# Five edits to a decoder layer's schedule: prepared weights, first differences, first sums, attention's merge, output steps

## The chip, the cores and the metric

The kernel runs on one core of a Trainium2 chip. The time is that of one execution of the whole program on the device, in microseconds. The engines that matter are TensorE (PE: matrix products and transposes), VectorE (DVE), ScalarE (ACT), GpSimd (POOL) and SyncE (SP), which here only issues transfers; ACT and POOL issue transfers too, between their computing instructions. [...]

## The reference

One layer of a decoder on 1024 positions of width 1024, in float32: half a SwiGLU block, a mixer of two groups of heads (stick-breaking attention and a Mamba-2 scan) side by side, cross-attention to 256 memory tokens, and a second half SwiGLU block, each between two RMS norms:

```
f = swiglu(rmsnorm(h, ffn1_pre_g), ffn1_w_gu, ffn1_w_down)
h = h + 0.5 * rmsnorm(f, ffn1_post_g)
m = hybrid_mixer(rmsnorm(h, mix_pre_g), w_in, ...)        # attention heads | SSD heads
h = h + rmsnorm(m, mix_post_g)
c = memory_cross_attention(rmsnorm(h, xa_pre_g), rmsnorm(mem, mem_g), ...)
h = h + rmsnorm(c, xa_post_g)
f = swiglu(rmsnorm(h, ffn2_pre_g), ffn2_w_gu, ffn2_w_down)
h = h + 0.5 * rmsnorm(f, ffn2_post_g)
```

## The kernel before

**Arithmetic.** Every float32 matrix is split into a high part (`hi`, a cast on ACT, L266) and a low part (`lo`, a subtraction on DVE, L268), and a product is three matmuls per block of 128 rows: high by high, high by low, low by high (`mm3`). The feed-forward blocks are computed with Strassen's seven products: `seven(f)` (L799) makes 7 products of 12 matmuls each for one tile `f` of the hidden width, in the order B22, B21, S1, S4, B12, S5, B11. The sums of weight blocks are formed on POOL (`wc`, L754), then split on ACT and DVE; their buffers (2 in the first block, 3 in the second) come free when the low part is made. Between the products the results are combined: ACT copies the first two (L808, L812), POOL subtracts them (L813), DVE adds the third to form `e` (L818). The sixth product, S5, accumulates in the bank that L818 reads, so PE starts it only after L818.

**The order of the work.** The program is written along PE's order. `clock` adds up the modelled cost of the matmuls traced so far, in ns; `later` is a list of steps with a due time on that clock, and `run_later` traces each step when PE's clock passes its time. A step traced in this way is kept behind the instruction traced just before it on its engine (`kp`). A scheduler then sets the final order of each engine. `merge(a, ta, b, tb)` interleaves two strands on PE: it advances `a` as long as (clock spent in a) / ta is not above (clock spent in b) / tb.

**Names and places that the change touches.**

- `prepare` (L191 on): weights for later stages are loaded in halves, split, and stored again as `dwhi` and `dwlo`, in steps `load`, `high` (ACT, L212), `low` (DVE, L216) and `store` (two transfers, L220). `prepare_all` (L241) sets the due times for 74 halves: one every 4300 from 152000 while below 416000 (62 halves), the other 12 every 9000 from 420000. Times below 418000 use SP's queue, later ones POOL's.
- `pair_sums(f, ...)` (L637): five sums over the tiles f-1 and f are made on DVE (L643); each is stored by a transfer from ACT's queue (L645) that is due 2500 later. At f = 5 in the second feed-forward block the first of them is due 4000 later than elsewhere.
- `last(k)` (L723): in the first feed-forward block it splits the four matrices B12, one cast on ACT and one subtraction on DVE each. They are due at 0, 800, 1600 and 2400 after the start of the first `seven` (L922).
- In attention, `tail()` is the last head pair (scores, scans on DVE, transposes, products with the values) and `beside()` is the first part of the output projection followed by the values of the memory tokens (`memory_values`). L1901 merges them with 32500 and 21000 + 5200 * 6 = 52200. After it come two weight tiles of the output projection whose halves were prepared, and `mix_out`, which loads the attention's result (`oraw`), splits it (`ohi`, `olo`) and sums its squares (`asum`).
- In cross-attention, at step s = 6 (L2168), the softmax and value steps of one head are merged with the first eight steps of two output tiles (`out_parts`), with weights 6100 and 5200.

Of the kernel before, what the change touches and what calls it, by code (L numbers as in the profile page):

```python
# [10 lines left out]
F32 = mybir.dt.float32  # L11
# [14 lines left out]
MIXED = 6  # L26
# [21 lines left out]
class Kern:  # L48
# [142 lines left out]
    def prepare(self, names, raw, pairs, times, switch=float("inf")):  # L191


        nc = self.nc
        work = []
        for name, i in names:
            hl = tuple(self.tc.dram_tile([P, KT, P], F32R, name=self.nm(n)) for n in ("dwhi", "dwlo"))
            self.ready[name, i] = hl
            work += [(self.ap["w_" + name][i], hl, slice(4 * n, 4 * n + 4)) for n in range(2)]
        raws, parts = {}, {}  # L200

        def queue(n):
            return nc.sync if times[n] < switch else nc.gpsimd

        def load(n):
            pool, tag, bufs = raw[n % len(raw)]
            raws[n] = self.t(pool, [P, 4, P], F32, tag, bufs=bufs)
            self.kp(queue(n).dma_start(out=raws[n], in_=work[n][0][:, work[n][2], :]))

        def high(n):  # L210
            parts[n] = [self.t(pool, [P, 4, P], F32R, tag, bufs=bufs) for pool, tag, bufs in pairs[n % len(pairs)]]
            self.kp(nc.scalar.copy(parts[n][0], raws[n]))  # L212

        def low(n):
            hi, lo = parts[n]
            self.kp(nc.vector.tensor_tensor(out=lo, in0=raws.pop(n), in1=hi.bitcast(F32), op=ALU.subtract))  # L216

        def store(n):
            for d, x in zip(work[n][1], parts.pop(n)):
                self.kp(queue(n).dma_start(out=d[:, work[n][2], :].bitcast(F32), in_=x.bitcast(F32)))  # L220

        if len(pairs) > 2:
            steps = ((low, -1, 0), (store, -2, 0), (high, 0, 0), (load, 2, 0))
        else:
            steps = ((high, 0, 0), (low, 0, 1200), (load, 2, 2400), (store, 0, 3000))
        times = list(times)[: len(work)]
        assert len(times) == len(work), (len(times), len(work))
        d = times[1] - times[0]
        times = {n: t for n, t in enumerate(times)}
        times.update({-n: times[0] - d * n for n in (1, 2)})  # L230
        times.update({len(work) + n: times[len(work) - 1] + d * (n + 1) for n in range(2)})
        for n in sorted(times):
            for f, m, dt in steps:
                if 0 <= n + m < len(work):
                    self.later.append((times[n] + dt, lambda f=f, m=n + m: f(m)))

# [4 lines left out]
    def prepare_all(self, sp):  # L241
        names = [("ssd", i) for i in [*range(6), *range(12, 26)]] + [("qkv", i) for i in range(QKV)]
        pairs = [
            ((self.fp, "acc0", None), (self.fp, "acc1", None)), ((self.fp, "rpost", None), (self.tp, "dg", None)),
            ((sp, "bh", None), (sp, "bl", None)),
        ]
        raw = [(sp, "braw", 2), (sp, "braw", 2), (self.xp, "xl0", KT + 1), (self.xp, "xl1", KT + 1)]
        n = 2 * len(names)
        a = [152000 + 4300 * i for i in range(n)]
        k = sum(t < 416000 for t in a)  # L250
        self.prepare(names, raw, pairs, a[:k] + [420000 + 9000 * i for i in range(n - k)], 418000)

    def wsrc(self, name, i):
        return self.ready[name, i] if (name, i) in self.ready else self.ap["w_" + name][i]
# [306 lines left out]
    def up_phase(self, sp, sp2, wgu, gpre, act_d, bank, load, plain, sizes, rw=None, begin=None):  # L561

        nc = self.nc
# [10 lines left out]
        if begin:  # L574
            x = sums(F32)
# [15 lines left out]
        xs_d, stored, later_sums, held = {}, [0] * (NFF // 2), [], []  # L591
# [45 lines left out]
        def pair_sums(f, even, odd):  # L637

            (t0, t1), (u0, u1) = even, odd
            j, c = f // 2, self.clock + (4000 if f == 5 and not begin else 0)  # L640

            def combine(n, out, a, b, op):
                self.kp(nc.vector.tensor_tensor(out=out, in0=a, in1=b, op=op))  # L643
                xs_d[n, j] = self.tc.dram_tile([P, H], F32, name=self.nm("xs"))
                at(self.clock + 2500, lambda: self.kp(nc.scalar.dma_start(out=xs_d[n, j], in_=out)))  # L645

            def fresh(n, a, b, op):
                combine(n, self.t(ftp, [P, H], F32, "cb", bufs=3), a, b, op)

            if c == self.clock:  # L650
                fresh("s6", t1, t0, ALU.subtract)
            else:
                at(c, fresh, "s6", t1, t0, ALU.subtract)
            at(c + 1500, fresh, "s5", t0, u0, ALU.add)
            at(c + 5000, combine, "s1", t0, t0, u1, ALU.add)
            at(c + 6500, combine, "s7", u0, u0, u1, ALU.subtract)
            at(c + 8000, combine, "s2", t1, t1, u1, ALU.add)
# [81 lines left out]
        def at(t, f, *args):  # L739
            self.later.append((t, lambda: f(*args)))  # L740
# [111 lines left out]
        t0, dt = (T0 + 12000, 7000) if begin else (T0 + 31000, 6500)  # L852
# [66 lines left out]
                        at(self.clock + 1000, next, Wb)  # L919
        for k in range(4):  # L920

            at(self.clock + (800 * k if begin else 1500 * k + 500), last, k)  # L922
        for f in range(first_seven, NFF):
            seven(f)
        if not begin:
# [662 lines left out]
    def attention(self):  # L1588
        nc, ap = self.nc, self.ap
        with self.pools("at", ["o", "a"], ["w"]) as (op, sp, wsp, pp):  # L1590
# [12 lines left out]
            begin = self.t(op, [P, S], BF16, "begin")  # L1603
# [4 lines left out]
            for hh in range(2):  # L1608
                nc.vector.tensor_scalar(
                    out=sc[:, 4 * hh : 4 * hh + 4], in0=self.C[hh], scalar1=-0.125, scalar2=None, op0=ALU.mult  # L1610
# [268 lines left out]
            def tail():  # L1879
                yield from units(7)  # L1880
                yield from values(*pend.pop())
                yield from drain(0)

            def beside():
                late.append(mix_row(1))
                self.first = self.mix_first(ready.pop())
                for n in range(4 * MIXED):
                    if n == 2:
                        late.pop()()
                    if n == 4 * MIXED - 4:  # L1890
                        ready.append(next(Wm))
                    next(self.first)
                    yield
                yield from memory_values(*mem_prep())
# [3 lines left out]
            self.Wo, self.mix_r, ready, late = self.wstream(wo[0:MIXED]), [], [], []  # L1898
            for p in range(7):
                self.merge(units(p), 24000, inproj(p + 1), 32500)  # L1900
            self.merge(tail(), 32500, beside(), 21000 + 5200 * MIXED)  # L1901
            self.Wo = self.wstream(wo[MIXED:])
            with self.pinned(self.clock + 2500):
                vout(*pend_v.pop(0))
# [123 lines left out]
    def xattn(self):  # L2028


        nc = self.nc
        with self.pools("xf", ["a", "b", "w"], []) as (sp, sp2, wsp, pp):
# [87 lines left out]
            def out_parts(k0, k1, n=2):  # L2120
                for i in range(n):
                    yield from out_part(ps[i], ws[i], 1, k0, k1)
# [11 lines left out]
            fill = qproj(1)  # L2134
# [3 lines left out]
            for s in range(8):  # L2138
                hh = s // 4
                if s == 2:  # L2140
                    self.resid(0, 4000)
                if s == 4:
                    self.F[0] = []
                    for d in range(8):
                        ps = self.t(self.mmp, [P, H], F32, "mm")
                        self.run_all(out_part(ps, next(W), 0, 0, 8))
                        out_copy(ps, 0)
                    self.run_later(float("inf"))
                    self.post(0, "xa_post_g", None, "ffn2_pre_g", step=5000, at=(8500, 16000, 19000))
                if s == 3:  # L2150
                    self.run_later(self.clock)
                if s + 2 < 8:
                    load(K, s + 2, "k", 2, 0)
                if s == 6:
                    self.resid(1, 4000)
                if s == 2:
                    self.flush(1)
                    self.later.append((self.clock + 10000, self.held.pop()))
                    self.prepare([("gu2", i) for i in range(2 * PLAIN[1])], *self.prep_pool(wsp), [self.clock + 9000 + 6000 * i for i in range(4 * PLAIN[1])])
                if s < 7:  # L2160
                    step = zip_(values(s), scores(s + 1))
                    if s < 6:
                        fill = qproj(s + 2)
                        for _ in range(4):
                            next(fill)
                        self.merge(step, 6100, fill, 8300)
                    else:
                        self.F[1] = []  # L2168
                        ws = [next(W) for _ in range(2)]
                        ps = [self.t(self.mmp, [P, H], F32, "mm") for _ in range(2)]  # L2170
                        self.merge(step, 6100, out_parts(0, 4), 5200)
                    load(V, s + 1, "v", 1, 1)
            v = values(7)
            self.run_all(out_part(ps[0], ws[0], 1, 4, 6))
# [4 lines left out]
            for d in range(8):  # L2179
# [3 lines left out]
                else:  # L2183
                    x = self.t(self.mmp, [P, H], F32, "mm")
# [187 lines left out]
```

## Time and profile before

| | |
|---|---|
| time, median of 3 runs (lowest to highest) | 2639.64 us (2636.35 to 2641.0) |
| time of the profiled execution | 2638.67 us |
| its span, first to last instruction | 2636.9 us |
| busy ACT, share of the span | 1293.0 us, 49% |
| mean granted TensorE clock | 0.995 |
| transfers | 489.82 MB, mean 186 GB/s |

In the views below, a row of a timeline gives the start and the duration in us, the engine (a trailing q: a transfer is issued), the line of the kernel, the operation, the tiles as out<-in, the shape and the count; in brackets stands how long the engine sat idle before it, and what ended that. A row of the waits gives who waited for whom, the total in us, how often, and the longest. A row of the windows gives a stretch, its length, the busy time of each engine with its instruction count, the TensorE clock that was granted (1.00 is full), the busy share of the transfer engines and GB/s.

### The profile page before, as it was taken

What the parts mean: (1) busy time and instruction counts of PE and PEld (TensorE: products, weight loads), DVE (VectorE), ACT (ScalarE), POOL (GpSimd) and SP (SyncE); (2) the same over time, 40 slices, a digit from 0 to 9 for tenths busy, and PEclk for the clock granted to TensorE, in tenths of its full rate; (3) what the DMA queues carried; (4) which work ended last, traced back from release to release, by engine and by line L of the source; (5) the groups of instructions that cost most, each with busy time, mean ns of one, the idle gap of its engine ahead of it and who ended that gap; (6) DMA issues with size and microseconds to landing.
All of it is one profiled execution on the core that took longest, in us unless ns stands there. A gap on an engine that the chain in (4) does not pass through costs nothing. (4 is left out here: it accounts for less than half of the span.)

```text
span 2636.9 us, 36866 instructions
## 1 busy us (share of the span) xinstructions
PE 2586.9 (98%) x12850; PEld 2153.9 (82%) x12850; DVE 1981.5 (75%) x3044; ACT 1293.0 (49%) x2300; POOL 601.8 (23%) x717
## 2 busy tenths in 40 slices
PE   9999999999999999999999999999999999999999
PEld 7788888778777778888888887788878788888887
DVE  6778897769689784777777867767556888776777
ACT  7434444545356563555555645345554433333553
POOL 2555553110100001111111110101011555452000
PEclk9999999999999999999999999999999999999999
DMA  6558888875654226555555556547658453336554
GB/s 219 175 193 279 283 278 290 279 248 183 229 183 168 86 75 214 166 151 149 148 149 126 155 155 219 184 148 252 200 179 294 142 178 116 97 99 224 192 170 154
DMA packets 212970, 489.82 MB, mean 186 GB/s; under 512 B 26544, under 2 KB 35120, under 8 KB 212784
## 3 DMA queue, kind: packets, MB, share of 16 engines
q1 hardware_dynamic: 162896, 369.48, 42.9%
q0 software_dynamic: 26560, 75.52, 9.7%
q10 hardware_dynamic: 23328, 42.48, 4.3%
q8 instruction: 101, 1.65, 0.3%
q14 instruction: 85, 0.70, 0.1%
HBM read 327.46 MB, written 138.94 MB: 177 GB/s over the span
## 5 line engine op out<-in xcount | busy, mean ns | idle before, releaser
L139 PE MATMUL mm<-xh,whi 128*128 128x512 f32 x1320 | 520.9, 404 | 2.6 <-DVE xl L1929 1.6
L139 PE MATMUL mm<-xh,wlo 128*128 128x512 f32 x1272 | 488.7, 391 | 1.9 <-DMA wlo<-dwlo 1.9
L139 PE MATMUL mm<-xl,whi 128*128 128x512 f32 (+1 forms) x1252 | 486.6, 389 | 0.3 <-DVE xl L275 0.3
L139 PEld LDWEIGHTS mm<-xh,whi 128*128 128x128 f32 x1320 | 248.2, 188 | 44.9 <-issue 3.8
L139 PEld LDWEIGHTS mm<-xh,wlo 128*128 128x128 f32 x1272 | 238.8, 188 | 54.6 <-DMA wlo<-dwlo 2.3
L139 PEld LDWEIGHTS mm<-xl,whi 128*128 128x128 f32 x1252 | 236.2, 189 | 33.3 <-DVE xl L275 0.6
L1761 DVE TENSOR_TENSOR_SCAN nb<-nb,begin 128x128 f32<-128x128 f32 (+7 forms) x128 | 171.1, 1351 | 55.4 <-ACT nb L1757 54.7
L1757 ACT ACTIVATE nb<-z,scale 128x128 f32<-128x128 f32 (+2 forms) x192 | 107.7, 580 | 73.9 <-PE z L139 73.6
L268 DVE TENSOR_TENSOR wlo<-wraw,whi 128x1024 fp32r<-128x1024 f32 x70 | 85.4, 1221 | 55.8 <-ACT whi L266 55.6
L266 ACT CAST whi<-wraw 128x1024 fp32r<-128x1024 f32 (+1 forms) x87 | 84.0, 965 | 83.5 <-PE mm L139 55.3
L1778 POOL DMA_DIRECT2D mix<-sq x64 | 52.9, 826 | 227.4 <-DVE sq L1776 180.7
L139 PE MATMUL dn<-xh,wlo 128*128 128x512 f32 x296 | 101.8, 392 | 2.0 <-DMA wlo<-dwlo 2.0
L661 ACT ACTIVATE ft<-ft 128x512 f32<-128x512 f32 x88 | 55.5, 632 | 97.2 <-DVE ft L660 95.2
L754 POOL TENSOR_TENSOR wc<-wraw,raw 128x512 f32<-128x512 f32 x56 | 79.8, 1425 | 65.8 <-DVE whi L268 19.5
L754 POOL TENSOR_TENSOR wc<-raw,wraw 128x512 f32<-128x512 f32 x55 | 80.3, 1459 | 51.6 <-DVE blk L268 21.6
L268 DVE TENSOR_TENSOR atl<-tr,ath 128x512 fp32r<-128x512 f32 (+1 forms) x106 | 66.4, 630 | 28.6 <-ACT ath L266 28.2
L839 POOL TENSOR_TENSOR ft<-ft,e 128x512 f32<-128x512 f32 x37 | 59.4, 1606 | 121.4 <-DVE e L838 45.0
L139 PE MATMUL mm<-ath,v 128*128 128x256 f32 x320 | 85.3, 289 | 0.0
L139 PE MATMUL dn<-xh,blk 128*128 128x512 f32 x264 | 85.2, 389 | 0.0
L266 ACT CAST whi<-wc 128x512 fp32r<-128x512 f32 x80 | 49.7, 621 | 71.1 <-PE dn L139 25.9
L266 ACT CAST wlo<-wc 128x512 fp32r<-128x512 f32 x79 | 49.1, 621 | 72.0 <-PE dn L139 27.2
L139 PE MATMUL dn<-xh,whi 128*128 128x512 f32 x240 | 83.9, 394 | 0.0
(584 smaller groups left out, 6811.2 us busy)
## 6 DMA issues: line engine op xcount, KB each, us to landing
whi<-dwhi SPq DMA_DIRECT2D x82, 512.0 KB, 3.6
wlo<-dwlo SPq DMA_DIRECT2D x82, 512.0 KB, 4.9
wraw<-in_w_gu SPq DMA_DIRECT2D x43, 512.0 KB, 4.3
raw<-in_w_gu SPq DMA_DIRECT2D x37, 512.0 KB, 4.2
dwhi<-bh SPq DMA_DIRECT2D x66, 256.0 KB, 4.1
dwlo<-bl SPq DMA_DIRECT2D x66, 256.0 KB, 4.3
wraw<-xs SPq DMA_DIRECT2D x56, 256.0 KB, 3.1
xs<-ft ACTq DMA_DIRECT2D x54, 256.0 KB, 3.4
```

The lines of the kernel that those rows point to most:

```text
L139: self._pe(self.nc.tensor.matmul(out, lhsT, rhs, start=start, stop=stop, skip_group_check=self.more), cost)
L266: self.kp(self.nc.scalar.copy(hi, src))
L268: self.nc.vector.tensor_tensor(out=lo, in0=src, in1=hi.bitcast(F32), op=ALU.subtract)
L661: nc.scalar.activation(t, t, AF.Silu)
L754: nc.gpsimd.tensor_tensor(out=t, in0=a, in1=b, op=op)
L839: nc.gpsimd.tensor_tensor(out=t1, in0=t1, in1=e, op=ALU.mult)
L1757: nc.scalar.activation(nb[:, s0:s1], z[:, 0:n], AF.Sigmoid, scale=sc[:, i : i + 1])
L1761: nc.vector.tensor_tensor_scan(out=nb[:, 0:Wd][:, ::-1], data0=nb[:, 0:Wd][:, ::-1], data1=begin[:, S - Wd : S][:, ::-1], initial=0.0, op0 ...
L1778: nc.gpsimd.dma_start(out=self.mix_d[p][a * 64 : a * 64 + 64, csl], in_=o, accum_op=ALU.add)
```

## The change

Five places are edited; no operation of the computation is added or left out.

1. A prepared half's two stores become two steps. For the 12 halves after 416000 (now 9) the second store is due 3000 after the first and the next load 6000 after; before that, and in the preparations with two buffer pairs, the order is as it was. The spacing becomes 4100 instead of 4300 (65 halves), then 12000 instead of 9000.
2. The transfers of the sums at f = 5 of the second feed-forward block are due 5000 after their sums instead of 2500.
3. The four splits of B12 in the first feed-forward block are due at 3000, 4500, 6000 and 7500 after the start of the first `seven`.
4. Attention's last merge weighs `tail()` with 26000 instead of 32500.
5. At s = 6 of cross-attention two of the eight output steps are traced ahead of the merge, and the rest is weighed with 4000.

```diff
-        def store(n):
-            for d, x in zip(work[n][1], parts.pop(n)):
-                self.kp(queue(n).dma_start(out=d[:, work[n][2], :].bitcast(F32), in_=x.bitcast(F32)))
+        def st0(n):
+            store(n, 0)
+
+        def st1(n):
+            store(n, 1)
+
+        def store(n, i):
+            d, x = work[n][1][i], parts[n][i]
+            self.kp(queue(n).dma_start(out=d[:, work[n][2], :].bitcast(F32), in_=x.bitcast(F32)))
 
         if len(pairs) > 2:
-            steps = ((low, -1, 0), (store, -2, 0), (high, 0, 0), (load, 2, 0))
+            steps = ((low, -1, 0), (st0, -2, 0), (st1, -2, 3000), (high, 0, 0), (load, 2, 6000))
         else:
-            steps = ((high, 0, 0), (low, 0, 1200), (load, 2, 2400), (store, 0, 3000))
+            steps = ((high, 0, 0), (low, 0, 1200), (load, 2, 2400), (st0, 0, 3000), (st1, 0, 3000))
...
         for n in sorted(times):
             for f, m, dt in steps:
+                if len(pairs) > 2 and times[n] < switch:
+                    dt = 0
...
-        a = [152000 + 4300 * i for i in range(n)]
+        a = [152000 + 4100 * i for i in range(n)]
         k = sum(t < 416000 for t in a)
-        self.prepare(names, raw, pairs, a[:k] + [420000 + 9000 * i for i in range(n - k)], 418000)
+        self.prepare(names, raw, pairs, a[:k] + [420000 + 12000 * i for i in range(n - k)], 418000)
...
-            j, c = f // 2, self.clock + (4000 if f == 5 and not begin else 0)
+            j, wait = f // 2, (5000 if f == 5 and not begin else 2500)
+            c = self.clock + (4000 if wait == 5000 else 0)
...
-                at(self.clock + 2500, lambda: self.kp(nc.scalar.dma_start(out=xs_d[n, j], in_=out)))
+                at(self.clock + wait, lambda: self.kp(nc.scalar.dma_start(out=xs_d[n, j], in_=out)))
...
-            at(self.clock + (800 * k if begin else 1500 * k + 500), last, k)
+            at(self.clock + (3000 + 1500 * k if begin else 1500 * k + 500), last, k)
...
-            self.merge(tail(), 32500, beside(), 21000 + 5200 * MIXED)
+            self.merge(tail(), 26000, beside(), 21000 + 5200 * MIXED)
...
-                        self.merge(step, 6100, out_parts(0, 4), 5200)
+                        fill = out_parts(0, 4)
+                        for _ in range(2):
+                            next(fill)
+                        self.merge(step, 6100, fill, 4000)
```

## The prediction

> **What bounds the kernel now.** I read the page's shares first, then PE's waits over the whole execution, then the granted clock of short stretches.
>
> ```profile
> span 2636.9 us, 36866 instructions
> PE 2586.9 (98%) x12850; PEld 2153.9 (82%) x12850; DVE 1981.5 (75%) x3044; ACT 1293.0 (49%) x2300; POOL 601.8 (23%) x717
> ```
>
> TensorE is the bound: 50.0 us of the span are not busy. The diff removes no matmul, so it can only shorten PE's waits, and stretches in which PE runs at a lower clock. The waits at the five edited places:
>
> ```profile
> PE dn L139 <- DVE e L818: 5.9, 2, 5.6
> PE dn L139 <- ACT F L1079: 3.6, 1, 3.6
> PE mm L139 <- DVE e L818: 3.1, 2, 2.8
> PE dn L139 <- ACT F L1074: 2.7, 1, 2.7
> PE ms L139 <- DVE atl L268: 2.6, 1, 2.6
> PE tr L142 <- DVE p L2077: 2.2, 2, 1.2
> PE dn L139 <- ACT ohi L273: 2.0, 1, 2.0
> PE mm L139 <- DMA wlo<-dwlo: 1.9, 1, 1.9
> PE ms L139 <- DVE asum L1953: 1.4, 1, 1.4
> PE dn L139 <- DVE olo L275: 0.6, 2, 0.3
> ```
>
> By place, from the timeline: 5.6 at 100.5 us (first `seven`); 2.8 at 2102 (f = 5 of the second block); 2.7 at 484 and 3.6 at 550 (first down projection); 2.6, 1.9, 2.0, 0.6 and 1.4 between 1536 and 1600 (attention's end); 1.2 at 1918 (cross-attention). Behind most of them PE is slow for a while, as the windows show:
>
> ```profile
> 99.00:105.90 6.90, 5.40 (x13) 4.24 (x14) 6.90 (x9) 3.01 (x5) 4.52 (x4) 0.51 0.17 58
> 484.70:488.20 3.50, 3.50 (x9) 2.76 (x10) 3.50 (x7) 2.85 (x6) 0.00 (x0) 0.51 0.53 149
> 1600.80:1604.30 3.50, 3.50 (x9) 2.73 (x10) 3.50 (x7) 3.00 (x5) 0.00 (x0) 0.51 0.73 228
> 2102.60:2106.10 3.50, 3.50 (x11) 2.69 (x9) 3.50 (x6) 0.63 (x1) 2.58 (x2) 0.51 0.05 19
> 1536.00:1539.50 3.50, 2.82 (x24) 2.83 (x25) 1.78 (x4) 1.39 (x4) 0.00 (x0) 1.00 0.52 150
> 152.00:416.00 264.00, 264.00 (x1166) 218.62 (x1165) 226.59 (x299) 118.91 (x207) 153.73 (x99) 1.00 0.76 262
> 416.00:484.00 68.00, 65.92 (x291) 54.24 (x289) 51.31 (x77) 32.68 (x58) 13.44 (x15) 1.00 0.94 326
> 1564.00:1596.00 32.00, 27.77 (x152) 23.09 (x150) 16.48 (x26) 13.90 (x24) 5.22 (x9) 1.00 0.94 316
> ```
>
> The column ahead of the last two is the granted clock. At 0.51, 3.5 us lose 3.5 × 0.49 = 1.7; the 5.40 busy us behind the longest wait lose 2.6. The 2.6 us wait at 1536 was followed by full clock, so a wait of that size stands at the edge. Between 152 and 416 us PE is never idle: 264.00 us for 1166 matmuls, 0.226 us each. All touched places together: 5.6 + 2.6 at 100; 2.8 + 1.7 at 2102; 2.7 + 3.6 + 2 × 1.7 = 9.7 in the down projection (two clock losses); 2.6 + 1.9 + 2.0 + 0.6 + 1.4 + 1.7 = 10.2 at attention's end; 1.2 at 1918. That is 33.8 us, the most that can be won directly.
>
> **Part by part: splits of B12 (edit 3).** The timeline before the 5.6 us wait, start and duration first:
>
> ```profile
> 89.89 0.68 DVE L268 TENSOR_TENSOR xl<-braw,xh 128x512 fp32r<-128x512 f32 x1
> 90.71 0.63 ACT L266 CAST wlo<-wc 128x512 fp32r<-128x512 f32 x1
> 91.70 0.68 DVE L268 TENSOR_TENSOR xl<-cb,xh 128x512 fp32r<-128x512 f32 x1
> 92.30 0.68 DVE L268 TENSOR_TENSOR wlo<-wc,wlo 128x512 fp32r<-128x512 f32 x1
> 93.06 1.68 POOL L754 TENSOR_TENSOR wc<-raw 128x512 f32<-128x512 f32 x1 [4.24 <-DVE wlo L268]
> 95.92 1.72 POOL L813 TENSOR_TENSOR sq<-sq,sq 128x512 f32<-128x512 f32 x1
> 96.43 1.75 DVE L268 TENSOR_TENSOR blk<-wraw,blk 128x512 fp32r<-128x512 f32 x1
> 99.77 0.68 DVE L818 TENSOR_TENSOR e<-sq,dn 128x512 f32<-128x512 f32 x1
> ```
>
> PE waits for `e` (99.77), which stands behind the low parts of weight sums in DVE's queue; those stand behind POOL, which had idled 4.24 us for a buffer that the low part at 92.30 frees. Ahead of that low part DVE makes the four `xl` of B12, 89.89 to 91.70: 0.60 us apart, 4 × 0.60 = 2.4. Due at 3000 to 7500, all four fall behind it, and B12 is read only by the fifth product, so POOL starts 2.4 earlier. Everything behind moves with it: the wait becomes 3.2, and the clock loss one usual 1.7 less a part of it (1.3 of the 2.6 goes): −3.7. Ends: the whole place, −8.2; or the four lows run beside POOL, where the low at 96.43 takes 1.75 instead of 0.68 us: 4 × 1.07 − 2.4 = +1.9. I take −3.7, nearest to the rows as they stand. [...]
>
> **Stores of first sums (edit 2).** At 2102:
>
> ```profile
> 2094.66 1.62 POOL L839 TENSOR_TENSOR ft<-ft,e 128x512 f32<-128x512 f32 x1 [2.67 <-ACT blk L266]
> 2096.24 3.42 POOL L754 TENSOR_TENSOR wc<-raw 128x512 f32<-128x512 f32 x2
> 2099.63 1.71 POOL L813 TENSOR_TENSOR sq<-sq,sq 128x512 f32<-128x512 f32 x1
> 2100.67 0.62 ACT L266 CAST whi<-wc 128x512 fp32r<-128x512 f32 x1 [3.71 <-DVE cb L643]
> 2101.38 0.69 DVE L818 TENSOR_TENSOR e<-sq,mm 128x512 f32<-128x512 f32 x1 [1.16 <-POOL sq L813]
> ```
>
> The store of `cb` holds ACT's queue 3.71 us for the sum, and the edit frees it. But `e` is released by POOL's L813, and POOL works from 2094.66 to 2101.34 (2099.63 + 1.71) without a gap. Value 0: POOL hides it. If ACT's casts were the true releaser, −4.5 (2.8 + 1.7). If the later stores keep a `cb` buffer 2.5 us longer and DVE's next sum stands in front of `e`, +2.5.
>
> **Attention's merge (edit 4).** I replayed the order that the rule of L1901 gives, each step by its count of matmuls (0.226 us for 512 columns, half for 256). With 32500 the tail ends 7.1 us before the stage; with 26000 the output projection and the memory values go ahead, and the tail ends last, its 16 last products with only 2 us of other work before them. The memory's weights are asked for and used about 4 us earlier in the stage.
>
> ```profile
> L139 PE MATMUL mm<-atl,v x56: 276/283/287, 1475.0 to 1563.2; 128*128 128x256 f32 x56
> 1570.45 0.59 SPq L182 DMA_DIRECT2D wlo<-dwlo  x1
> L268 DVE TENSOR_TENSOR atl<-tr,ath 128x512 fp32r<-128x512 f32 (+1 forms) x106 | 66.4, 630 | 28.6 <-ACT ath L266 28.2
> raw<-in_w_gu SPq DMA_DIRECT2D x37, 512.0 KB, 4.2
> ```
>
> (a) At 1536 a row product waits for a bank that an `atl` reads. In the replay it comes 2.6 instead of 0.8 us behind the transposes into that bank: −1.8. (b) The weights asked for at 1570.45 land 3.9 later; such a load lands in 4.2 (last row). Issued 4 us earlier against the first use, its wait goes, up to a rest where the transfer engines are 0.94 busy: −1.7 of 1.9. (c) `oraw`, `ohi`, `olo` and `asum` follow on the same queues: I let −1.9 of 2.6 and −0.7 of 1.4 go, since a share of 0.94 leaves little room. (d) The clock loss at 1600.8 goes with them: −1.5 of 1.7. (e) New: the last transposes of the tail are followed by their cast and `atl` (0.63 by its row, and about as much for the cast) and then products with 2 us of cover; I charge +1.5. Sum −6.1. Ends: −10.2 with all gone; +3.2 where nothing goes and the tail's last chain is uncovered twice over (1.5 + 1.7 clock loss).
>
> **Output steps in front (edit 5).** At 1918:
>
> ```profile
> 1917.35 1.21 DVE L268 TENSOR_TENSOR wlo<-wraw,whi 128x1024 fp32r<-128x1024 f32 x1
> ```
>
> A transpose waits 1.2 for `p`, which stands behind this low part on DVE. Two steps, 6 matmuls × 0.226 = 1.36 us, now stand ahead of it: −1.1. Ends −1.2 and, if the steps are missed at the end of the merge, +1.2.
>
> **Prepared weights (edit 1).** Up to 416 us: 264 / 4.1 against 264 / 4.3 gives 3 more halves of 768 KB where PE has no wait: 0. After it, 9 halves instead of 12, with the stores apart. The two waits hang on late weights:
>
> ```profile
> 545.04 0.69 DVE L1022 TENSOR_TENSOR cb<-wraw,xl 128x512 f32<-128x512 f32 x1 [2.19 <-DMA wraw<-in_w_dn]
> SPq L220 <- DVE dg L216: 38.8, 12, 10.7
> ```
>
> A weight transfer now stands behind one piece of 256 KB instead of three; at the 326 GB/s of 416 to 484 us a piece takes 0.8. That moves the 550 wait by at most 1.6, and I take half: −0.8. The 484 wait is ACT's own queue and stays. Ends: −9.7 (both with their clock), and +8.3 (the slower rival's single event below).
>
> Sum: −3.7 + 0 − 6.1 − 1.1 − 0.8 = −11.7. The profiled execution took 2638.67 (span 2636.9 and 1.8 around it), 0.97 under the median of 2639.64, so the forecast is 2638.67 − 11.7 = 2627.0.
>
> **Rivals.** *The orders resolve their places fully.* Edit 3 brings −8.2 and edit 4 −7.8 (as above without the two rests, 0.2 and 1.5), edit 5 −1.2, edit 1 −0.8, edit 2 −4.5: −22.5, 2616. For it: a wait below 2.6 brings no clock loss, so gains double near that edge. Against: POOL's gapless row at 2094.66.
>
> *VectorE and GpSimd slow each other.* The B12 lows run beside POOL and give edit 3 back (+1.9): −11.7 + 3.7 + 1.9 = −6.1, 2632.6. For it: 1.75 at 96.43; against: POOL's idle 4.24 shows that there was room. [...]
>
> *Nothing much happens.* Edit 4's stretch is bound by its transfers (0.94) and gives 0; edit 3 moves only two splits past the low part, −1.2; edit 5 −1.1: 2636.4.
>
> *Slower: prepared stores hold the weight queue.* SP's queue takes its transfers in order, and between 152 and 416 us it held 12 times for the low part of a prepared half (last row above), up to 10.7 us. Weight loads of the feed-forward stand behind those stores. At 4100 they fall at other points of the 84-matmul tile (84 × 0.226 = 19.0 us). Two longest holds in a row, 21.4, and 4.2 of landing exceed the 19.0 by 6.6; with 1.7 of clock loss that is 8.3 an event. From two longest holds back to back on it decides. Three such events, +24.9 − 11.7: 2651.9. For it: the denser spacing and the DMA share of 0.76; against: 264.00 us without one wait.
>
> **How the numbers follow.** Forecast 0.36 (its own range 2618 to 2634); full resolution 0.16; contention 0.10; nothing much 0.16; slower 0.22 (with one event 2635, three 2652). About 0.2%, or 5.3 us, can be told from no change: faster 0.36 + 0.16 + 0.10 = 0.62, same 0.16, slower 0.22. The range reaches from below the full resolution (2616, less 7 of the down projection's 9.7) to 2648, between two and three events, and leaves out about half of the slower case and little below.
>
> **What would show it.** Edit 3: POOL's idle 4.24 before the sum at 93 us shrinks and the wait for `e` falls to about 3; wrong if the lows of B12 take 1.75 beside POOL and the wait stays. Edit 2: the ACT idle of 3.71 goes, the 2.8 wait stays. Edit 4: the waits on `atl` at 1536, `wlo<-dwlo` and `ohi` go, the window near 1600 shows clock 1.00, a new wait on `ath` or `atl` stands at the tail's end. Edit 5: the wait for `p` is one of 1.0 instead of two. Edit 1: the wait for F at 484 stays, that at 550 shrinks, and PE stays at 264.00 of 264; a wait there for a weight with half a clock behind it would prove the slower rival. A time above 2634 makes the forecast wrong.

## The result

The changed kernel takes 2633.28 us, median of 12 runs (2630.33 to 2640.5); the kernel before took 2640.61 us in 12 runs beside them. The ratio is 0.9976, 95% interval 0.9967 to 0.9985: faster by 4.0 to 8.7 us. The forecast was 2627.0, 11.7 us under the profiled run, with its likeliest own range 2618 to 2634. The time lies just inside that range, but the gain, 7.3 us by the medians and 6.3 by the ratio, is little more than half of what was forecast: the sign was right, the size was not, and the parts were off by more than the sum shows. Two executions took several times as long (8137 us of e_first_without_b12, 12882 us of the kernel before beside it); without them the medians that stand below as 2633.33 and 2641.47 are 2632.99 and 2641.05.

The page of the changed kernel, and then the waits of TensorE over the whole execution (who waited for whom, total in us, how often, longest). Lines after the edits are 8 to 12 higher: L827 is the old L818, L1083 and L1088 the old L1074 and L1079, L2086 the old L2077.

```profile
span 2628.6 us, 36857 instructions
PE 2584.9 (98%) x12850; PEld 2152.0 (82%) x12850; DVE 1988.5 (76%) x3044; ACT 1292.8 (49%) x2300; POOL 595.9 (23%) x708
```

```profile
PE dn L139 <- DVE e L827: 5.9, 2, 5.7
PE mm L139 <- DVE e L827: 3.3, 2, 2.8
PE dn L139 <- ACT F L1088: 3.1, 1, 3.1
PE dn L139 <- ACT F L1083: 2.8, 1, 2.8
PE mm L139 <- DVE xl L276: 1.7, 3, 0.7
...
PE dn L139 <- DVE olo L283: 1.6, 2, 1.0
...
PE tr L142 <- DVE p L2086: 1.3, 1, 1.3
```

The wait for `e` near 100 us is 5.7 where it was 5.6, although edit 3 was to shorten it, and 1.7 of waits for `xl` are new. The waits at 484 and 550 us are 2.8 and 3.1. The waits on `atl` (2.6), `wlo` (1.9), `ohi` (2.0) and `asum` (1.4) have left the top of the list. The wait for `p` occurs once instead of twice.

Where the time went can be read from the start of the same matmul, counted from the first one, in both traces (changed less before). The places lie where the order of TensorE is the same in both; edit 4 changes it from 1480 to 1572 us, edit 5 from 1915 to 1928 us.

| stretch of the kernel before, us | gained (-) or lost (+), us | edit there |
|---|---|---|
| 0 to 50 | -0.7 | none |
| 50 to 150, first `seven` | +2.05 | 3 |
| 150 to 456 | 0.0 | 1 (4100) |
| 456 to 568, first down projection | -0.4 | 1 (12000, stores apart) |
| 568 to 1476 | +0.3 | none |
| 1476 to 1622, attention's end | -6.0 | 4 |
| 1622 to 1691 | -2.3 | none |
| 1691 to 1903 | 0.0 | none |
| 1903 to 1968 | -1.1 | 5 |
| 1968 to the end | 0.0 | 2 |

The sum is -8.3, the difference of the spans. The -0.7 at the start, ahead of every edit, shows how far two executions differ by themselves. The windows of the changed kernel (stretch, length, busy time of TensorE, weight loads, VectorE, ScalarE, GpSimd with counts, granted clock, transfer share, GB/s):

```profile
100.10:106.90 6.80, 4.53 (x11) 3.57 (x12) 6.63 (x8) 2.22 (x4) 3.72 (x4) 0.50 0.42 152
1591.70:1595.10 3.40, 3.27 (x8) 2.48 (x8) 3.40 (x6) 2.14 (x4) 0.00 (x0) 0.50 0.45 142
2093.50:2096.80 3.30, 2.94 (x7) 2.36 (x8) 3.30 (x5) 0.00 (x0) 1.69 (x2) 0.50 0.28 109
152.00:416.00 264.00, 264.00 (x1166) 218.63 (x1165) 231.51 (x300) 120.88 (x212) 152.36 (x99) 1.00 0.79 269
```

Half clock (0.50) still follows the waits near 100 and 2093 us (and those at 484 and 550 us, with 0.50 from 485.8 and from 550.7), and one still falls at attention's end, now at 1591.7. Between 152 and 416 us TensorE is busy all the 264.00 us again.

The timeline of the changed kernel around the first `seven` (start, duration, engine; in brackets the idle time before and what ended it):

```profile
90.01 0.68 DVE L276 TENSOR_TENSOR wlo<-wc,wlo 128x512 fp32r<-128x512 f32 x1
...
90.76 1.66 POOL L763 TENSOR_TENSOR wc<-raw 128x512 f32<-128x512 f32 x1 [1.83 <-DVE wlo L276]
...
91.21 1.77 DVE L276 TENSOR_TENSOR xl<-rpost,xh 128x512 fp32r<-128x512 f32 x1
...
93.66 1.67 POOL L763 TENSOR_TENSOR wc<-raw,wraw 128x512 f32<-128x512 f32 x1 [1.23 <-DVE blk L276]
94.10 1.77 DVE L276 TENSOR_TENSOR xl<-cb,xh 128x512 fp32r<-128x512 f32 x1
...
95.28 1.73 POOL L822 TENSOR_TENSOR sq<-sq,sq 128x512 f32<-128x512 f32 x1
...
95.80 1.76 DVE L276 TENSOR_TENSOR blk<-wc,blk 128x512 fp32r<-128x512 f32 x1
...
97.48 0.68 DVE L276 TENSOR_TENSOR blk<-wraw,blk 128x512 fp32r<-128x512 f32 x1
...
98.08 1.75 DVE L276 TENSOR_TENSOR whi<-wc,whi 128x512 fp32r<-128x512 f32 x1
...
99.96 1.76 DVE L276 TENSOR_TENSOR wlo<-wc,wlo 128x512 fp32r<-128x512 f32 x1
...
101.64 0.68 DVE L827 TENSOR_TENSOR e<-sq,dn 128x512 f32<-128x512 f32 x1
```

The first half went as forecast: the low part is at 90.01 instead of 92.30, GpSimd idles 1.83 instead of 4.24 and starts its sum 2.3 earlier. But two of the four moved `xl` lows now run beside GpSimd and take 1.77, so VectorE works from 90.01 on almost without a gap. GpSimd's subtraction is done at 97.01 (95.28 + 1.73), and yet `e` starts at 101.64: three lows stand in front of it in VectorE's queue, at 97.48, 98.08 and 99.96, the last of which stood behind `e` before.

### The profile page after: what moved, and what is told of

Read it like the earlier page. It is cut to its first block, busy times and chain, and to the rows that moved or that the text cites. A ratio compares the mean times of both kernels' runs of the same rounds, so it can differ in the third digit from the quotient of the medians.

```text
span 2628.6 us, 36857 instructions
## 1 busy us (share of the span) xinstructions
PE 2584.9 (98%) x12850; PEld 2152.0 (82%) x12850; DVE 1988.5 (76%) x3044; ACT 1292.8 (49%) x2300; POOL 595.9 (23%) x708
## 5 line engine op out<-in xcount | busy, mean ns | idle before, releaser
L274 ACT CAST ath<-tr 128x512 fp32r<-128x512 f32 (+1 forms) x108 | 58.9, 546 | 55.0 <-PE tr L142 50.7
L139 PE MATMUL mm<-atl,v 128*128 128x256 f32 x320 | 82.7, 281 | 0.7 <-DVE atl L276 0.7
```

What stands on the lines that cost most here:

```text
L139: self._pe(self.nc.tensor.matmul(out, lhsT, rhs, start=start, stop=stop, skip_group_check=self.more), cost)
L274: self.kp(self.nc.scalar.copy(hi, src))
```

## The experiments

All are timed in several runs; the ratio is to the kernel before, in runs on the same chip.

| run | median us (runs) | ratio, 95% interval |
|---|---|---|
| changed kernel | 2633.28 (12) | 0.9976, 0.9967 to 0.9985 |
| b12_only | 2643.26 (12) | 1.0006, 0.9996 to 1.0016 |
| merge_only | 2634.14 (11) | 0.9974, 0.9964 to 0.9984 |
| without_b12 | 2630.66 (7) | 0.9961, 0.9947 to 0.9975 |
| prep_only | 2637.02 (12) | 0.9985, 0.9976 to 0.9995 |
| e_first_with_b12 | 2632.38 (7) | 0.9968, 0.9956 to 0.9981 |
| e_first_without_b12 | 2633.33 (7) | 0.9969, 0.9958 to 0.9981 |
| first_subtraction_on_vector | 2631.99 (5) | 0.9963, 0.9949 to 0.9977 |
| f5_subtraction_on_vector | 2630.10 (5) | 0.9957, 0.9944 to 0.9970 |
| e_first_b12_loads_on_act | 2630.31 (5) | 0.9968, 0.9956 to 0.9981 |
| e_first_no_b12_loads_on_act | 2628.97 (5) | 0.9961, 0.9949 to 0.9974 |
| prep_spacing_only | 2634.85 (11) | 0.9985, 0.9976 to 0.9993 |
| prep_apart_only | 2637.22 (11) | 0.9992, 0.9983 to 1.0001 |

The median of before was 2640.98 beside the first four experiments, 2641.47 beside the next four and 2638.75 beside the last four.

### Edit 3 alone, and the changed kernel without it

```diff
-            at(self.clock + (800 * k if begin else 1500 * k + 500), last, k)
+            at(self.clock + (3000 + 1500 * k if begin else 1500 * k + 500), last, k)
```

> The kernel before with edit 3 alone (the splits of B12 due at 3000 to 7500). Theory (the lows run beside GpSimd, and e falls one low part further back in VectorE's queue): +2.1 us against before, about 2642.7; TensorE waits some 1.7 us for xl between 91 and 96 us, and the wait for e near 102 us stays at 5.6 to 5.7. Rival (the loss at that place in the changed kernel came from the start of the program, which began otherwise there, and the splits themselves are worth the forecast -3.7): 2637, and the wait for e is about 3.2.

2.3 us slower by the medians (2643.26 against 2640.98). The interval, 1.1 us faster to 4.2 slower, does not hold the forecast gain of 3.7. In its trace the wait for `e` is 5.7 and one wait for `xl` of 0.6 is new, so the rival's 3.2 did not come; nor did the 1.7 for `xl`. Between 50 and 150 us this trace takes as long as that of before (+0.1 us); most of the 5.6 us by which it is longer lie between 456 and 568 us (+2.6) and between 1622 and 1691 us (+2.2), where edit 3 changes nothing.

> The changed kernel with edit 3 taken back. Theory: 2.1 us faster than the changed kernel, 10 us faster than before, about 2630.5. Rival (edits 1, 2, 4 and 5 lose elsewhere what the splits hid): the same time as the changed kernel, 2633.

2630.66, 2.6 us under the changed kernel by the medians and 4.0 by the ratios (0.9976 - 0.9961 = 0.0015 of 2640). The two intervals overlap by 0.0008, some 2 us. The two runs together show that edit 3 did not bring its 3.7. By the medians each puts its cost at 2 to 3 us, but neither makes it certain, and at the edit's own place one trace shows +2.05 and the other +0.1: whether it costs anything stays open. The place varies by itself: with the old splits the wait for `e` was 5.6 in the profile of before and 4.2 here.

### Edit 4 alone

```diff
-            self.merge(tail(), 32500, beside(), 21000 + 5200 * MIXED)
+            self.merge(tail(), 26000, beside(), 21000 + 5200 * MIXED)
```

> The kernel before with edit 4 alone (26000 in place of 32500). Theory (all of the gain between 1513 and 1691 us is this edit's): -8.5 us, about 2632, of it 6.2 up to 1622 us and 2.3 at the wait for wlo near 1663 us with its half clock. Rival (the 2.3 behind 1622 us came from the place of the windows of the clock, which moved with everything ahead of them, not from the merge): -6.2 us, about 2634.4, with the half clock near 1668 us still there.

6.8 us faster (2634.14 against 2640.98; the interval says 4.2 to 9.5). The same matmul starts 2.6 later than in before at 1476 us and 3.2 earlier at 1622: 5.8 gained there. Of the 2.3 behind it, only 0.9 appears: the wait for `wlo` at 1663 is there with 2.7 us, with full clock behind it (1.00 from 1666.4 to 1669.8). The waits of TensorE in attention's end of this run:

```profile
PE ms L139 <- DVE asum L1953: 1.7, 1, 1.7
PE dn L139 <- DVE olo L275: 1.3, 2, 0.7
PE mm L139 <- DVE xl L1929: 1.3, 1, 1.3
PE mm L139 <- DVE atl L268: 0.7, 1, 0.7
...
PE ms L139 <- DVE atl L268: 0.3, 1, 0.3
```

The long waits on `atl`, `wlo` and `ohi` are gone; the new one on `atl`, 0.7, is the tail's uncovered end. So the gain up to 1622 us is the merge's alone, as the theory had it. The 2.3 behind it is not the merge's, as the rival had it, though the half clock that the rival expected there did not come: three traces without edit 4 show a gain there too (1.9 in prep_only and prep_spacing_only, 3.2 in prep_apart_only).

### Edit 1: alone, and each half of it

The whole edit is the first part of the diff above, everything up to `prepare_all`.

> The kernel before with edit 1 alone (prepared weights 4100 apart, stores apart after 416 us). Theory: nothing, within 1 us of before, 2640.6; TensorE's wait at 484 us stays at 2.7 to 2.9, that at 550 us shrinks by about half a microsecond, and something like 0.5 is lost near 665 us. Rival (the stores apart let weights land earlier): the wait at 550 us goes with its half clock, -5.3 us, 2635.3.

4.0 us faster by the medians (2637.02 against 2640.98), 1.3 to 6.3 by the interval: the theory's "nothing" fell, and so did the rival's picture, since the wait at 550 us is still 3.0. The wait at 484 us fell to 2.2. The mean clock from 470 to 570 us is 0.98, against 0.97 in before; by an estimate (3.4 us at 0.50 are 0.017 of these 100) that is one half clock less, where two stand in before. Of the 4.2 us by which this trace is shorter than that of before, 2.0 lie between 456 and 568 us and 1.9 between 1622 and 1691 us, where no half is prepared: there the wait for `wlo` is 1.7 instead of 2.0.

```diff
-        a = [152000 + 4300 * i for i in range(n)]
+        a = [152000 + 4100 * i for i in range(n)]
...
-        self.prepare(names, raw, pairs, a[:k] + [420000 + 9000 * i for i in range(n - k)], 418000)
+        self.prepare(names, raw, pairs, a[:k] + [420000 + 12000 * i for i in range(n - k)], 418000)
```

> The kernel before with only the spacing of the prepared halves (4100 and 12000), both stores and the load at one due time as before. Edit 1 alone gained 4.0 us where 0.8 was forecast. Theory (fewer halves after 416 us, 9 in place of 12 and farther apart, leave ScalarE and the transfers to the first down projection): most of it, -3, about 2638; the waits at 484 and 550 us sum to 5.3 or less against 6.3 in the profile of before. Rival (the stores apart do it): within 1 us of 2641.

3.9 us faster (2634.85 against 2638.75; 1.8 to 6.3): the spacing alone brings what the whole edit brings, though its one trace shows the two waits at 3.5 and 2.8, 6.3 in sum as in before and not the 5.3 expected, and it gains nothing between 456 and 568 us (+0.2), but 1.9 between 1622 and 1691 us.

```diff
-            steps = ((low, -1, 0), (store, -2, 0), (high, 0, 0), (load, 2, 0))
+            steps = ((low, -1, 0), (st0, -2, 0), (st1, -2, 3000), (high, 0, 0), (load, 2, 6000))
```

> The kernel before with only the second store 3000 and the load 6000 behind the first store after 416 us, the spacing as before (4300 and 9000). Theory (spacing): within 1 us of 2641. Rival (stores apart): -3 to -4, about 2637.5.

1.5 us faster by the medians, 0.3 slower to 4.5 faster by the interval: not told from nothing. What one trace of each says of the place, with the matmuls that TensorE started between 470 and 570 us:

| trace | preparations | waits at 484 and 550 us | matmuls |
|---|---|---|---|
| before | old | 2.7, 3.6 | 399 |
| b12_only | old | 3.4, 4.5 | 387 |
| merge_only | old | 3.3, 4.6 | 388 |
| prep_only | new | 2.2, 3.0 | 408 |
| without_b12 | new | 3.1, 2.5 | 408 |
| changed kernel | new | 2.8, 3.1 | 401 |
| prep_spacing_only | new spacing | 3.5, 2.8 | 398 |
| prep_apart_only | stores apart | 1.9, 4.0 | 400 |

The profile on which the forecast rested shows the old preparations better than the two other traces with them, in which 12 and 11 fewer matmuls are started, 2.7 and 2.5 us at 0.226 each. Each new form shows 398 to 408, so which half of the edit does it, and how much of the 4.0 is won at this place, is argued and not shown. A single profile did not show what there was to win at this place.

### `e` put in front

The lows of the next weight pieces are kept behind `e` on VectorE (`self._after`; `low` is the subtraction that `split` now returns):

```diff
+            if begin and f == first_seven:
+                self.behind = first_e.ins
...
+                if begin and f == first_seven + 1 and i >= 1:
+                    self._after(low.ins, self.behind)
```

> The changed kernel (edit 3 in), with the three lows that stood ahead of e in VectorE's queue in the first seven (pieces 8, 9 and 10) put behind it. Theory (edit 3 lost through the order: with the four xl lows moved, one more low fell ahead of e): e runs at 97.5 instead of 101.6 us, TensorE's wait of 5.7 falls to about 1.5, -4.1 and -1.7 to -3.4 of half clock, about 2626.5. Rival (the loss is VectorE and GpSimd taking turns, whatever the order): e moves, but the lows behind it keep the next products waiting, -1 at most, 2632.5.

> The same order of e, with edit 3 taken back. Theory (order): e behind GpSimd's subtraction at 97.7, -2.1 and one half clock of 1.7 against 2630.7, 2627; so edit 3 no longer costs anything against this, within 1 us. Rival (taking turns): edit 3 still costs 2 to 3 us between this run and the one before it.

2632.38 and 2633.33: neither time that the theory gave, though its picture at the place came true. The first is the time of its rival, but not by the rival's mechanism, as the timeline of the run with edit 3 shows:

```profile
97.06 0.67 DVE L829 TENSOR_TENSOR e<-sq,dn 128x512 f32<-128x512 f32 x1
...
97.79 3.02 PE L139 MATMUL dn<-S,wlo 128*128 128x512 f32 x12 [1.55 <-DVE e L829]
...
111.79 1.65 POOL L621 DMA_DIRECT2D cb<-act  x3
...
119.22 1.29 DVE L628 TENSOR_TENSOR xl<-cb,cb 128x512 f32<-128x512 f32 x2 [5.09 <-DMA cb<-act]
...
121.63 0.68 DVE L829 TENSOR_TENSOR e<-sq,mm 128x512 f32<-128x512 f32 x1
...
122.37 1.22 PE L139 MATMUL mm<-S,wlo 128*128 128x512 f32 x2 [5.24 <-DVE e L829]
```

`e` now runs at 97.06, and TensorE's wait is 1.55 instead of 5.71. But 24 us on, in the next `seven`, TensorE waits 5.24 us for that tile's `e`. It stands behind the first sums of an earlier pair, and these wait 5.09 us for loads that GpSimd issued at 111.79. In before the same loads had been waited for 3.5 us at 118 us, which nobody noticed, since TensorE was late by its wait at 100. The time that the first wait cost had paid for the second. Edit 3 costs nothing in this pair (0.9968 against 0.9969).

### The first subtraction on VectorE

```diff
-            nc.gpsimd.tensor_tensor(out=d, in0=d, in1=t5, op=ALU.subtract)
+            if begin and f == first_seven:
+                with self.urgent():
+                    nc.vector.tensor_tensor(out=d, in0=d, in1=t5, op=ALU.subtract)
+            else:
+                nc.gpsimd.tensor_tensor(out=d, in0=d, in1=t5, op=ALU.subtract)
```

> Edit 3 taken back, and in the first seven GpSimd's subtraction (sq minus sq) moved to VectorE, e right behind it and piece 7's low behind both. Theory (e hangs on GpSimd's queue and then on the lows): TensorE's wait of 4.2 to 5.6 near 100 us goes whole, with its half clock, -6 to -7.5 against 2630.7, about 2624. Rival (ACT's second copy, behind ACT's casts, is the last thing e needs): the wait only falls to about 2, and the time is about 2628.

2631.99, no faster than without_b12. The profiled execution, 2637.16, is the slowest of the five. In it the wait for `e` near 100 us is gone whole (one of 1.2 for ScalarE's copy stands ahead of it), and the one in the next `seven`, where VectorE again waits 5.3 us for the loads of the first sums, is 6.7, of 11.0 in all such waits:

```profile
PE mm L139 <- DVE e L833: 11.0, 4, 6.7
```

### The loads of the first sums issued by ScalarE

```diff
-            act_sums(later_sums.pop(0), self.clock)
+            act_sums(later_sums.pop(0), self.clock, nc.scalar if begin and f == 4 else nc.gpsimd)
```

> As e_first_with_b12 (edit 3 in, e ahead of three lows), and the four loads of the first sums at f = 4 issued by ScalarE instead of GpSimd. Theory (in e_first_with_b12 the wait near 100 us went and a wait of 5.2 came at 122 us, because VectorE waited 5.1 us for loads that GpSimd issued and that took 6.1 us to land; one lag of the helpers, showing at the next place): VectorE's wait for these loads goes, TensorE's wait at 122 us falls below 1.5, its half clock of 6.8 us goes, some -6 us against 2632.4, about 2626.5. Rival (the lag is that of the weight chain through GpSimd and VectorE, and the loads only happened to be last): the wait at 122 us stays over 3, within 2 us of 2632.4.

> The same without edit 3. Theory: the wait of 4.8 at 121 us goes as well, and what is left is the wait of 2.7 near 97 us: about 2627, so edit 3 with e in front is as good or up to 1.5 us better. Rival (edit 3 costs 2 to 3 us in any order): this is 2 to 3 us faster than the run before it.

2630.31 and 2628.97. TensorE's waits between 86 and 124 us in the first of the two:

```profile
PE dn L139 <- DVE e L829: 1.6, 1, 1.6
PE mm L139 <- DVE xl L275: 1.1, 3, 0.7
PE mm L139 <- DVE e L829: 1.1, 1, 1.1
```

The wait in the next `seven` falls from 5.2 to 1.1: those loads were what it hung on, and not the weight chain. Of the 6 expected, the time falls by 2.1 by the medians, and not at all by the ratios, each to the kernel before beside it (0.9968 both); in the traces the stretch from 50 to 150 us is 3.2 us shorter. In the profiles part of the rest is the clock: full (1.00) behind the wait at 97 us in e_first_with_b12, it is half (0.50) there in this run (below). Without edit 3 the time is 1.3 us lower still, with waits of 2.8 near 97 us and 2.1 in the next `seven`, where the theory expected the second to go. So whether edit 3 costs anything once `e` stands in front (0 in the pair above, 1.3 in this one, intervals that overlap) stays open.

### The subtraction at f = 5 on VectorE

The same diff, with `not begin and f == 5` as its condition.

> Edit 3 taken back, and GpSimd's subtraction at f = 5 of the second block moved to VectorE. It tests the reason for costing edit 2 at nothing. Theory (GpSimd's gapless work holds e at 2102 us): the wait of 2.8 goes with its half clock, -4.5 against 2630.7, about 2626. Rival (e is held by VectorE's own queue, the low and the sum ahead of it): the wait stays over 2, within 1 us of 2630.7.

2630.10, 0.6 us under without_b12, which can't be told from nothing. The timeline:

```profile
2089.64 1.77 DVE L276 TENSOR_TENSOR blk<-wraw,blk 128x512 fp32r<-128x512 f32 x1
...
2091.34 0.68 DVE L652 TENSOR_TENSOR cb<-ft,ft 128x512 f32<-128x512 f32 x1
2091.94 0.68 DVE L831 TENSOR_TENSOR e<-sq,mm 128x512 f32<-128x512 f32 x1
...
2092.67 4.53 PE L139 MATMUL mm<-S,whi 128*128 128x512 f32 x12 [2.20 <-DVE e L831]
```

The wait falls from 2.8 to 2.2 only. In before VectorE had stood idle for 1.16 us ahead of this `e`, so GpSimd was the last releaser. Here VectorE has the subtraction to do as well (1.78 us), and the low part and the first sum stand ahead of `e` without a gap. The time is the rival's, but the run does not show that VectorE's queue held `e` before; it shows that this queue comes next.

### The same stretches in all traces

The stretches of the table in the section on the result, measured in the same way in all fourteen traces, one for each kernel (us against before, which counts as 0):

| stretch, us | traces with the edit (how many) | traces without it |
|---|---|---|
| 50 to 150, edit 3, the rest of this place as in before | +0.1 and +2.05 (2) | -1.6 to +0.6 (7) |
| 456 to 568, edit 1 whole | -2.0 to +1.9 (9) | 0 to +2.6 (3) |
| 1476 to 1622, edit 4 | -6.3 to -3.9 (9) | -1.0 to +0.5 (5) |
| 1622 to 1691, no edit; by edit 1, whole or half | -3.4 to +0.6 (11) | -0.9 to +2.2 (3) |
| 1903 to 1968, edit 5 | -1.1 in each (9) | -0.1 to +0.1 (5) |
| 1968 to the end, edit 2 alone | -0.1 to +0.5 (8) | -0.1 to +1.0 (5) |

Edits 2 and 5 had no run of their own, but edit 5 gains its 1.1 in each of nine traces and in none without it, and edit 4 gains in each of nine. Edit 3 gains in neither of its two. For edit 1 the ranges overlap at both places, and only three traces have the old preparations: where its 4.0 us are won stays open.

## Why the prediction was off, point by point

**Splits of B12 (-3.7; measured +2.05 in the changed kernel's trace, +0.1 at the same place alone, +2.3 alone by the medians).** This is the step that failed. "Everything behind moves with it" took the chain from the low part through GpSimd to `e` as the only order that counts. GpSimd's sum did move by 2.3, but `e` is released by VectorE's own queue, in which the four moved lows still have to run, two of them at 1.77 instead of 0.68, and one further low came ahead of `e`. The rows of before had shown this order: GpSimd's subtraction ended at 97.64 (95.92 + 1.72), and `e` started at 99.77, 2.1 us later, behind the low at 96.43 and one more that the prediction left out:

```profile
98.10 1.75 DVE L268 TENSOR_TENSOR whi<-wc,whi 128x512 fp32r<-128x512 f32 x1
```

What came is what the prediction had named as the sign of being wrong here. The end that was put at +1.9 (lows beside GpSimd) points the right way, and the price per slowed low, 1.07, fits: 1.77 - 0.68 = 1.09. That +1.9 lies so close to +2.05 is luck: it charged four slowed lows, where two were slowed and the further low made up the rest. That the order mattered is shown by e_first_with_b12, where the wait near 100 us is 1.55. That shortening the wait there wins little is shown by the same run: the second wait behind it was missed altogether. No run that shortened the wait near 100 us came near the -8.2 of the other end.

**Stores of first sums (0; measured 0).** Right in size; the wait at 2093 is 2.8 as before. The reason was incomplete: GpSimd hides the edit, and VectorE's queue would hide it next (f5_subtraction_on_vector took 0.6 of the 2.8). ScalarE's idle of 3.71, which was to go, fell to 2.03.

**Attention's merge (-6.1; measured -6.0, alone -5.8 in its trace and -6.8 by the medians).** Right in size. In pieces: the wait at 1536 went whole (2.6 where 1.8 was expected), that on `wlo` too (1.9 for 1.7), the tail's new end costs 0.8 (0.7 on `atl`, 0.1 on `ath`) where 1.5 was charged; `ohi`, `olo` and `asum` together gave 2.2 (4.0 in before, 1.6 + 0.2 now) where 2.6 was booked; but the half clock did not go, it moved to 1591.7 (0.50), where -1.5 was booked. The errors cancel; that the sum came out so well is in part luck.

**Output steps in front (-1.1; measured -1.1).** Right, and the wait for `p` is one instead of two.

**Prepared weights (-0.8; -4.0 alone by the medians, -0.4 in the pair of profiles).** The sign was right, the size of the term was not: a fifth of what the edit brings. The forecast priced one piece of a transfer at one wait, from a profile in which this place stood better than usual, and left the half clocks behind both waits out; that the wait at 484 us would stay did not hold in prep_only (2.2 instead of 2.7). Where the rest of the 4.0 is won stays open.

**The sum.** With each edit's own measure it is 2.3 - 6.8 - 4.0 - 1.1 = -9.6, against -7.3 by the medians of the changed kernel; each measure has an interval of about 2.5 us to either side, so nothing more needs to be found. The forecast lost 6.0 on the splits and missed 3.2 on the preparations, so the two errors hide each other in part. Of the rivals, the slowing of VectorE and GpSimd by each other, with 2632.6, came nearest, in part by its own mechanism and in part by luck, since it kept the -0.8 for the preparations. The trace of the changed kernel speaks for it: a low beside GpSimd's sum at 90.76 takes 1.77 us, where others take 0.68. The slower rival did not occur: 264.00 of 264.00 us busy at the closer spacing.

**The best version.** Without edit 3 the kernel takes 2630.66. f5_subtraction_on_vector, with 2630.10 and the lowest ratio, and e_first_no_b12_loads_on_act, with 2628.97 and the lowest median, can't be told from it. All three have lower medians than both kernels.

## What to carry to other kernels

A wait that is removed can show the next lateness of the same helpers, which it had paid for (here 5.71 us fell to 1.55, and 5.24 came one tile on): before a gain is booked, look one tile further, at helpers' idle times that nobody waited for. When the releaser of an instruction moves, its own queue can be the next bound (here `e` ran at 101.64 with its input done at 97.01, behind three lows): count what stands ahead of it there, at the durations that hold beside the other engine (1.75 to 1.77 us instead of 0.68). A wait after which the clock may or may not fall (1.00 behind 2.7 us in merge_only, 0.50 behind 1.0 and 0.7 in the changed kernel) needs several profiles before a price is put on it.

## What the hardware showed

**A wait of a given length cost half a clock in one run and none in another.** These two runs have the same waits behind the same work near 97 us (1.1 to 1.2 for `xl`, then 1.55), and the same 3.4 us behind them, e_first_with_b12 first:

```profile
97.80:101.20 3.40, 3.40 (x15) 2.82 (x16) 3.40 (x4) 1.15 (x2) 2.17 (x2) 1.00 0.00 0
```

```profile
97.60:101.00 3.40, 3.40 (x8) 2.72 (x9) 3.40 (x4) 1.14 (x2) 2.17 (x2) 0.50 0.36 130
```

Fifteen matmuls are started in one and eight in the other. In the same way merge_only kept full clock (1.00) behind a wait of 2.7 us that ended at 1666 us, and the changed kernel got half a clock (0.50) at 1591.7 behind two waits of 1.0 and 0.7. Merge_only, the stretch with the wait and the one behind it:

```profile
1663.00:1666.40 3.40, 0.70 (x4) 0.26 (x2) 0.69 (x1) 0.42 (x1) 0.54 (x1) 1.00 1.00 345
1666.40:1669.80 3.40, 3.40 (x15) 2.79 (x16) 0.87 (x2) 0.00 (x0) 0.00 (x0) 1.00 0.50 202
```

So the edge near 2.6 us that the prediction read from one trace is none, and in that trace itself half clock, 0.50 from 1669.15 us, followed a wait of 2.0 for `wlo`. What decides whether a wait costs half a clock was not shown. How long the half clocks are and where they lie was: in before those at 484.73, 549.58 and 1600.88 us last 3.41 us each, and the one at 99.02, behind the longest wait, lasts 6.83, twice that. Their starts are 385.71, 64.85 and 1051.31 us apart, which is 113, 19 and 308 times 3.413 to within 0.03. In the changed kernel those that start at 100.05, 485.76, 550.61 and 1591.68 lie 385.71, 64.85 and 1041.07 apart, 113, 19 and 305 times 3.413; the first starts 1.03 us later than in before. By an estimate from these figures, one half clock of 3.41 us more or less, at 0.50, moves a profile by 1.7 us.

**VectorE's lows were slowed beside GpSimd's sums.** Of VectorE's lows between 90 and 102 us in the changed kernel, those that start while a GpSimd sum runs take 1.75 to 1.77 us, and the others 0.68, also where a sum starts while they run. A slowed low ends 0.54 to 0.56 us after the sum beside it, as if it had waited for that sum: 92.98 against 92.42, 95.87 against 95.33, 97.56 against 97.01. GpSimd's own instructions there take 1.26 to 1.73. So the two lows that edit 3 moved into the time of GpSimd's sums were not free there: 1.77 us each instead of 0.68.
